# Five-product blocks of a gate and up projection: a bank of its own for the fourth product, ScalarE instead of VectorE on the running sum, and less urgent weights

## The chip, the cores and the metric

The kernel runs on one core of one Trainium2 chip. The metric is device time in microseconds (us) for one execution of the whole program. The core has a matrix engine (TensorE), a vector engine (VectorE, DVE in the rows), a scalar engine (ScalarE, ACT), GpSimd (POOL) and SyncE (SP), whose queue issues the DMAs. Matrix products land in PSUM, eight banks of 128 x 512 float32; everything else that is computed on lies in SBUF.

## The reference

Two layers of an encoder on x of 1024 tokens by 1024 features, all in float32. Each layer projects x, runs three groups of heads side by side (a gated linear recurrence, retention, and 2-D neighbourhood attention), projects their outputs back and normalises; then comes the part that the larger half of the change concerns:

```
hid = silu(x @ w_gate[l]) * (x @ w_up[l])
x = layer_norm(ALPHA * x + hid @ w_down[l])
```

w_gate and w_up are 1024 x 2816, that is 22 blocks of 128 hidden features. The other part of the change touches the recurrent group: six heads of 64 channels in three blocks of 128 channels, each with an x projection, a gate projection, a convolution of width four and two recurrences.

## The kernel before

**Products.** Each float32 matrix is split into an upper half, rounded to the matrix engine's float32r, and the rest; a product of two matrices is three matmuls (upper x upper, upper x rest, rest x upper). Each split is one ScalarE copy (`hi`, line 119) and one subtraction (`lo`, line 122) on VectorE, now and then on GpSimd.

**Gate and up.** `gate_up` computes x @ w_gate and x @ w_up by Strassen's scheme in Winograd's form, on 2 x 2 blocks: the token halves, the feature halves, and hidden blocks j and j + 11. So there are eleven pairs j, each with a w_gate and a w_up block, and each block has seven products of 12 matmuls (128 x 128 by 128 x 512). The left operands are sums of weight blocks: GpSimd forms them (`lefts`, line 902), ScalarE and VectorE split them into tiles `wsp`. The right operands B11, B21, B22, T1 to T4 are sums of quarters of x. In a name such as `w_gate<-T1h,wsp` the right operand tells the product: T2 is product 6, T3 is 7, T1 is 5, T4 is 4, B22 is 3.

For the first four pairs (`EARLY`) products 1 and 2 are done ahead, in `two`, while the last right operands are still being made; product 1 is kept in SBUF in `first[j]`, called `p1` in the rows. `rest` then does the last five products of these pairs, in the order 6, 7, 5, 4, 3, and all seven of pairs 4 to 10. In `rest`, products 6, 5 and 3 add up in one bank `z["a"]`, which is read in between:

```
p6: product 6 into a;         21 = p1 + a
p7: product 7 into d
p5: product 5 on to a;        22 = p1 + a; 22 = 22 + d
p4: product 4 on to d;        21 = 21 + d
p3: product 3 on to a;        12 = p1 + a
```

The additions are the `add` of line 1035, on VectorE. In pairs 4 to 10 product 1 is in bank a already, and 21 and 22 are copied out by ScalarE (line 1065). As each sum is complete, `done` hands it on: a gate's sum goes through a Silu on ScalarE (line 1136), an up's sum is multiplied with it on VectorE (line 1141, `hid`) and sent to DRAM. After the pair's last sum, four combinations for the down projection follow on VectorE (line 902, `hs` and `hid`). GpSimd also forms four sums of w_down per pair (line 1017, `qt`), sent to DRAM as `wt`.

**Order of work.** The program is traced as a list, and a planner then orders each engine's instructions beforehand: among those that it holds ready by its own estimate of durations, the one traced earliest goes first. `high_priority(offset=n)` makes instructions count as traced n earlier. Each engine then works through its list strictly in order. The weights of a block are prepared (`prep`) before the products of the block ahead of it are traced.

**Buffers.** PSUM has eight banks in rings: `mm` two (bank d), `mx` three (bank a), `mo` one, `ml` two. In SBUF, `W` has ten tiles (split weights, and `p1`), `wraw` four (loaded weights), `Q` four (GpSimd's sums), `S` eight (sums on their way, among others).

**The start of a layer.** `wload` loads a weight and splits it, the split with an urgency of `rush` = 400. `layer` runs `lru_main(0)` (x and gate projections of the recurrent group's block 0), in layer 1 between the last transposes and splits of x (`catch_up`, tiles `x2h` and `x2l`). It then weaves `lru_main(1)` with `lru_mix(0)`, whose first step is block 0's convolution (lines 326 to 329, tile `xc`, split into `xch` and `xcl`, which the gates' matmuls `lg` read), and `lru_main(2)` with `lru_mix(1)`; the weights of `w_rv` come next.

Of the kernel before, what the change touches and what calls it, by code (L numbers as in the profile page):

```python
# [11 lines left out]
AF = mybir.ActivationFunctionType  # L12
# [27 lines left out]
def weave(*lists):  # L40

    todo = []
    for n, st in enumerate(lists):
        st = [s if isinstance(s, tuple) else (1, s) for s in st]
        total, at = sum(c for c, _ in st), 0
        for i, (c, f) in enumerate(st):
            todo.append(((at + c / 2) / total, n, i, f))
            at += c
    for t in sorted(todo, key=lambda t: t[:3]):
        t[3]()  # L50


class Trunk:
    def __init__(self, ctx, tc, a):
        self.tc, self.nc, self.a = tc, tc.nc, a
        pool = lambda name, bufs, **kw: ctx.enter_context(tc.tile_pool(name=name, bufs=bufs, **kw))
        self.cp = pool("cp", 1)
        self.xp = pool("xp", 8)
        self.tp = pool("tp", 18)
        self.qp = pool("qp", 4)  # L60
        self.wp = pool("wp", 10)
        self.sp = pool("sp", 8)
        self.mp = pool("mp", 8)
        self.dp = pool("dp", 1, space=DRAM)
        self.pm = pool("pm", 1, space=PSUM)
        self.n = 0
        self.rush = 400
        self.rest = None


# [53 lines left out]
    def wload(self, src, n=1024):  # L124
        nc = self.nc
        raw = self.raw("wraw")
        nc.sync.dma_start(raw[:, :n], src)
        wh, wl = self.W("wh"), self.W("wl")
        with self.tc.high_priority(offset=self.rush):
            self.hi(wh[:, :n], raw[:, :n])  # L130
            self.lo(wl[:, :n], raw[:, :n], wh[:, :n])
        return wh, wl
# [661 lines left out]
    def layer(self, l):  # L794
        nc, tc, V, A = self.nc, self.tc, self.nc.vector, self.nc.scalar
        self.l = l
        ys = {}
        R, N, L = [{}, {}, {}], [{}, {}], [{}, {}, {}]
        m = self.lru_main(0, L[0])
        if l == 0:  # L800
            self.start(L[0])
            m = m[2:]
        for i, f in enumerate(m):
            f()
            self.catch_up(i)
        weave(self.lru_main(1, L[1]), self.lru_mix(0, L[0], ys))
        weave(self.lru_main(2, L[2]), self.lru_mix(1, L[1], ys))
        m = self.ret_main(0, R[0])
        weave(self.ret_v() + cost(0, [self.ret_tables]) + cost(2, m[:1]), cost(6, [lambda: None]) + self.lru_mix(2, L[2], ys))
        weave(m[1:])  # L810
        self.ret_tables2()
        weave(self.ret_main(1, R[1]), self.ret_mix(0, R[0], ys))
        if l == 0:
            self.bias()
        weave(self.ret_main(2, R[2]), self.ret_mix(1, R[1], ys))
        weave(self.na_v() + self.na_main(0, N[0]), self.ret_mix(2, R[2], ys))
        m = self.na_mix(0, N[0], ys)

        YH, YL = {}, {}
        ws = {}  # L820
        res = {}

        def ysplit(hf, i):
            def step():
                q, k = divmod(i, 4)
                if (hf, q) not in YH:
                    YH[hf, q], YL[hf, q] = self.X("yh"), self.X("yl")
                yh, yl = YH[hf, q][:, k, :], YL[hf, q][:, k, :]
                sl = slice(hf * 512, hf * 512 + 512)
                if i < 6:  # L830
                    t = self.S("yb")
                    nc.sync.dma_start(t, self.yd[i, :, sl])
                else:
                    t = ys[i][:, sl]
                self.hi(yh, t)
                self.lo(yl, t, yh)

            return step

        def load_res(tt):  # L840
            res[tt] = self.T("res")
            src = self.a["x"] if l == 0 else self.xd
            nc.sync.dma_start(res[tt], src[tt * P : (tt + 1) * P, :])

        def wout(chunks, evac):
            return [lambda tt=tt: wout_t(chunks, evac, tt) for tt in range(8)]

        def wout_t(chunks, evac, tt):
            if tt == 0:
                for i in chunks:  # L850
                    ws[i] = self.wload(self.a["w_out"][l, i * P : (i + 1) * P, :])
            hf, c = tt // 4, (tt % 4) * P
            if tt not in res:
                load_res(tt)
            for fh in range(2):
                ps = self.ps("wo", "mx" if fh and chunks is rest else "mm")
                f = slice(fh * 512, fh * 512 + 512)
                for j, i in enumerate(chunks):
                    for q, (y_, w_) in enumerate(((YH, 0), (YL, 0), (YH, 1))):
                        self.mm(ps, y_[hf, i // 4][:, i % 4, c : c + P], ws[i][w_][:, f], j == 0 and q == 0, j == len(chunks) - 1 and q == 2)  # L860
                evac(tt, f, ps)

        def ev0(tt, f, ps):
            with self.tc.high_priority(offset=self.rush):
                V.scalar_tensor_tensor(out=res[tt][:, f], in0=res[tt][:, f], scalar=ALPHA, in1=ps, op0=ALU.mult, op1=ALU.add)

        part, rest = (0, 1, 2, 3), (4, 5, 6, 7)
        wp = wout(part, ev0)
        nm = self.na_main(1, N[1])
        weave(nm[:2] + cost(0, [ysplit(0, i) for i in part]) + nm[2:] + wp[:2] + cost(0, [ysplit(1, i) for i in part]) + wp[2:6] + cost(0, [ysplit(hf, i) for hf in range(2) for i in (4, 5, 6)]) + wp[6:], m + self.na_mix(1, N[1], ys))  # L870
        for hf in range(2):
            for i in (7,):
                ysplit(hf, i)()
        g, b = self.gb(1)

        def ev1(tt, f, ps):
            with self.tc.high_priority(offset=self.rush):
                V.tensor_tensor(out=res[tt][:, f], in0=res[tt][:, f], in1=ps, op=ALU.add)
            if f.start:
                self.norm(res[tt], g, b, tt >= 4, tt < 7, then=lambda q: nc.sync.dma_start(self.x1d[tt * P : (tt + 1) * P, q], res[tt][:, q]))  # L880

        self.op = {}
        steps = wout(rest, ev1)
        for tt in range(8):
            steps[tt]()
            if tt == 7:
                self.settle()
            if tt >= 3:
                self.to_ops(tt - 3, res[tt - 3])
        self.gate_up([lambda t=t: self.to_ops(t, res[t]) for t in range(5, 8)])  # L890
        self.down()
# [84 lines left out]
    def gate_up(self, late):  # L976

        nc, l, V, A, G = self.nc, self.l, self.nc.vector, self.nc.scalar, self.nc.gpsimd
# [78 lines left out]
        def rest(name, j, w, done):  # L1057

            z = {}
            p1_ = first[j][:, NAMES.index(name), :] if j in first else None  # L1060

            def snap(n):
                z[n] = self.S(name + n)
                if p1_ is None:
                    A.activation(z[n], z["a"], AF.Copy)
                else:
                    add(z[n], p1_, z["a"])

            def p1():
                z["a"] = self.ps(name, "mx")  # L1070
                product(w, 1, z["a"], True)
                snap("11")

            def p2():
                b = self.ps(name, "mo")
                product(w, 2, b, True)
                add(z["11"], z["11"], b)
                done("11", z["11"])

            def p6():  # L1080
                if "a" not in z:
                    z["a"] = self.ps(name, "mx")
                product(w, 6, z["a"], p1_ is not None)
                snap("21")

            def p7():
                z["d"] = self.ps(name)
                product(w, 7, z["d"], True)

            def p5():  # L1090
                product(w, 5, z["a"], False)
                snap("22")
                add(z["22"], z["22"], z["d"])
                done("22", z["22"])

            def p4():
                product(w, 4, z["d"], False)
                add(z["21"], z["21"], z["d"])
                done("21", z["21"])

            def p3():
                product(w, 3, z["a"], False)
                if p1_ is not None:
                    snap("12")
                done("12", z.get("12", z["a"]))

            return ([p1, p2] if p1_ is None else []) + [p6, p7, p5, p4, p3]
# [309 lines left out]
```

## Time and profile before

| | |
|---|---|
| median of 3 runs | 2318.07 us (2317.54 to 2320.31) |
| the profiled execution | 2320.11 us |
| its span, first to last instruction | 2318.3 us |
| TensorE busy | 2241.5 us, 97% |
| VectorE, ScalarE, GpSimd busy | 1444.5, 983.9, 920.7 us |

A row of the profile names the line, the engine, the operation, the tile written and the tiles read, with their shapes. Matmuls are pipelined: one of 128 x 512 is shown with 0.39 us, while the next starts 0.23 us after it. Times of a row are microseconds from the start of the span.

### The profile page before, as it was taken

The page shows a single profiled execution, that of the slowest core. Times are in us where ns is not written, and L with a number is a line of the kernel's source. Part 1 is how long each engine was busy: PE and PEld are TensorE (multiplying, and loading weights), DVE is VectorE, ACT ScalarE, POOL GpSimd, SP SyncE. Part 2 cuts the span into 40 slices and gives each one's busy share as a digit, 9 for nine tenths or more (in the row PEclk, how much of TensorE's full clock was granted, in tenths as well). Part 3 has the DMA queues.
Part 4 walks back from the last instruction along what each step waited for, and adds up shares of the span by engine and source line. Part 5 has one row for each costly group of instructions (what it writes and reads, how often), then busy time and mean ns, then how long its engine had stood idle before and what let it go on. Part 6 is the DMA issues. An engine that isn't in the chain of part 4 may idle for free. (4 is left out here: it accounts for less than half of the span.)

```text
span 2318.3 us, 29337 instructions
## 1 busy us (share of the span) xinstructions
PE 2241.5 (97%) x10790; PEld 1811.2 (78%) x10790; DVE 1444.5 (62%) x2073; ACT 983.9 (42%) x1501; POOL 920.7 (40%) x568
## 2 busy tenths in 40 slices
PE   8999999999899999999989999999998999999998
PEld 6787877788678888888768878777876788888886
DVE  6966546588665666543658656456886665655336
ACT  5654355463223333444346533554632333343432
POOL 1425500045544343475513245001455443435655
PEclk9999999999999999999999999999999999999999
DMA  5232233324544445785321322333355454558742
GB/s 173 101 114 60 67 119 107 123 106 162 191 151 167 146 169 199 290 291 176 123 73 46 114 64 64 123 103 121 114 164 190 155 173 140 178 190 306 275 159 87
DMA packets 142697, 340.47 MB, mean 147 GB/s; under 512 B 24024, under 2 KB 37336, under 8 KB 142552
## 3 DMA queue, kind: packets, MB, share of 16 engines
q1 hardware_dynamic: 142552, 338.58, 43.4%
q8 instruction: 85, 1.39, 0.2%
q14 instruction: 60, 0.49, 0.1%
HBM read 242.88 MB, written 90.08 MB: 144 GB/s over the span
## 5 line engine op out<-in xcount | busy, mean ns | idle before, releaser
L116 PE MATMUL dn<-dw,hx 128*128 128x512 f32 x1848 | 420.7, 389 | 2.0 <-DVE dw L122 2.0
L116 PEld LDWEIGHTS dn<-dw,hx 128*128 128x128 f32 x1848 | 346.5, 188 | 74.3 <-DVE dw L122 2.4
L122 POOL TENSOR_TENSOR hx<-hraw,hx 128x1024 fp32r<-128x1024 f32 x80 | 206.5, 2597 | 196.6 <-ACT hx L119 193.1
L119 ACT ACTIVATE wsp<-qS 128x512 fp32r<-128x512 f32 x176 | 110.6, 631 | 276.0 <-PE w_up L116 136.1
L122 DVE TENSOR_TENSOR dw<-wraw,dw 128x1024 fp32r<-128x1024 f32 x84 | 122.5, 1464 | 159.4 <-ACT dw L119 149.7
L122 DVE TENSOR_TENSOR wsp<-qS,wsp 128x512 fp32r<-128x512 f32 x176 | 165.7, 942 | 65.6 <-ACT wsp L119 63.9
L119 ACT ACTIVATE dw<-wraw 128x1024 fp32r<-128x1024 f32 x84 | 83.1, 989 | 204.2 <-PE dn L116 188.0
L122 DVE TENSOR_TENSOR wl<-wraw,wh 128x1024 fp32r<-128x1024 f32 (+2 forms) x84 | 111.8, 1339 | 74.7 <-ACT wh L119 66.6
L119 ACT ACTIVATE wh<-wraw 128x1024 fp32r<-128x1024 f32 (+2 forms) x84 | 84.9, 1015 | 115.1 <-PE rk L116 27.7
L122 DVE TENSOR_TENSOR wsp<-wraw,wsp 128x512 fp32r<-128x512 f32 x100 | 110.7, 1110 | 23.0 <-ACT wsp L119 22.1
L902 POOL TENSOR_TENSOR qS<-wraw 128x512 f32<-128x512 f32 x44 | 65.0, 1477 | 142.6 <-DVE wsp L122 74.0
L119 ACT ACTIVATE wsp<-wraw 128x512 fp32r<-128x512 f32 x100 | 62.8, 630 | 129.9 <-PE w_up L116 81.0
L116 PE MATMUL wo<-wh,yh 128*128 128x512 f32 x256 | 103.0, 402 | 0.0
L116 PE MATMUL wo<-wl,yh 128*128 128x512 f32 x256 | 101.8, 398 | 0.0
L116 PE MATMUL wo<-wh,yl 128*128 128x512 f32 x256 | 100.7, 393 | 0.0
L1035 DVE TENSOR_TENSOR w_gate<-w_gate,w_gate 128x512 f32<-128x512 f32 x58 | 39.6, 682 | 91.2 <-PE w_gate L116 61.0
L119 ACT ACTIVATE hx<-hraw 128x1024 fp32r<-128x1024 f32 (+1 forms) x88 | 81.5, 940 | 16.6 <-DMA hraw<-hd 16.6
L642 POOL MEMSET tab<- 128x768 f32 x16 | 12.7, 794 | 182.0 <-DMA vd<-nv 46.9
L116 PE MATMUL w_gate<-T1h,wsp 128*128 128x512 f32 x176 | 64.5, 431 | 20.6 <-DVE w_gate L1035 17.3
L902 POOL TENSOR_TENSOR qS<-qS,wraw 128x512 f32<-128x512 f32 x44 | 67.3, 1529 | 41.0 <-issue 32.3
L902 POOL TENSOR_TENSOR qS<-wraw,wraw 128x512 f32<-128x512 f32 x44 | 60.7, 1379 | 57.3 <-DVE wsp L122 57.3
L1017 POOL TENSOR_TENSOR qt<-wraw 128x512 f32<-128x512 f32 x22 | 29.0, 1320 | 136.0 <-issue 122.1
(409 smaller groups left out, 6136.9 us busy)
## 6 DMA issues: line engine op xcount, KB each, us to landing
wraw<-in_w_down_dram SPq DMA_DIRECT2D x74, 512.0 KB
hraw<-hd SPq DMA_DIRECT2D x66, 512.0 KB
wraw<-in_w_gate_dram SPq DMA_DIRECT2D x52, 512.0 KB
wraw<-in_w_up_dram SPq DMA_DIRECT2D x52, 512.0 KB
wt<-qt SPq DMA_DIRECT2D x88, 256.0 KB
hd<-hid SPq DMA_DIRECT2D x80, 256.0 KB
wraw<-wt SPq DMA_DIRECT2D x40, 512.0 KB
wraw<-in_w_st_dram SPq DMA_DIRECT2D x36, 512.0 KB
```

The source lines that it names most:

```text
L116: return self.nc.tensor.matmul(out, lhsT=lhsT, rhs=rhs, start=start, stop=stop, skip_group_check=more)
L119: return self.nc.scalar.activation(out, src, AF.Copy, scale=scale)
L122: return (eng or self.nc.vector).tensor_tensor(out=out, in0=src, in1=hi.bitcast(F32), op=ALU.subtract)
L642: self.order(nc.gpsimd.memset(t, NEG), self.mark)
L902: t = lambda o, x, y, op: eng.tensor_tensor(out=o, in0=x, in1=y, op=op)
L1017: t = lambda o, x, y: G.tensor_tensor(out=o, in0=x, in1=y, op=ALU.subtract)
L1035: add = lambda o, x, y: V.tensor_tensor(out=o, in0=x, in1=y, op=ALU.add)
```

## The change

In the five-product form of `rest` (pairs 0 to 3 of each layer):

- the sum after product 6 and the one after product 5 are copied out of bank a by ScalarE without p1;
- p1 is added to bank d after product 7, on VectorE, into a new tile q of the ring `S`, and q is then added to 22 and to 21;
- product 4 starts a bank of its own, the one called `mo`, and 21 takes in q and then that bank;
- 12 = p1 + a stays on VectorE.

Besides, `wload` takes its urgency from a new number, `rushw`, which is 40 instead of 400 while `lru_main(1)` and `lru_mix(0)` are traced; for all other weights it stays at 400.

```diff
-        self.rush = 400
+        self.rush = self.rushw = 400
...
-        with self.tc.high_priority(offset=self.rush):
+        with self.tc.high_priority(offset=self.rushw):
             self.hi(wh[:, :n], raw[:, :n])
             self.lo(wl[:, :n], raw[:, :n], wh[:, :n])
...
+        self.rushw = 40
         weave(self.lru_main(1, L[1]), self.lru_mix(0, L[0], ys))
+        self.rushw = 400
         weave(self.lru_main(2, L[2]), self.lru_mix(1, L[1], ys))
...
             def snap(n):
                 z[n] = self.S(name + n)
-                if p1_ is None:
-                    A.activation(z[n], z["a"], AF.Copy)
-                else:
-                    add(z[n], p1_, z["a"])
+                A.activation(z[n], z["a"], AF.Copy)
...
             def p6():
-                if "a" not in z:
+                if p1_ is not None:
                     z["a"] = self.ps(name, "mx")
                 product(w, 6, z["a"], p1_ is not None)
                 snap("21")
...
             def p7():
                 z["d"] = self.ps(name)
                 product(w, 7, z["d"], True)
+                if p1_ is not None:
+
+                    z["q"] = self.S("q")
+                    add(z["q"], p1_, z["d"])

             def p5():
                 product(w, 5, z["a"], False)
                 snap("22")
-                add(z["22"], z["22"], z["d"])
+                add(z["22"], z["22"], z["d"] if p1_ is None else z["q"])
                 done("22", z["22"])

             def p4():
-                product(w, 4, z["d"], False)
-                add(z["21"], z["21"], z["d"])
+                if p1_ is None:
+                    product(w, 4, z["d"], False)
+                    add(z["21"], z["21"], z["d"])
+                else:
+                    e = self.ps(name, "mo")
+                    product(w, 4, e, True)
+                    add(z["21"], z["21"], z["q"])
+                    add(z["21"], z["21"], e)
                 done("21", z["21"])

             def p3():
                 product(w, 3, z["a"], False)
                 if p1_ is not None:
-                    snap("12")
+                    z["12"] = self.S(name + "12")
+                    add(z["12"], p1_, z["a"])
                 done("12", z.get("12", z["a"]))
```

## Rows read from the trace of the kernel before

**Rows 1.** The page: busy time of each engine, its share of the span, instructions.

```profile
PE 2241.5 (97%) x10790; PEld 1811.2 (78%) x10790; DVE 1444.5 (62%) x2073; ACT 983.9 (42%) x1501; POOL 920.7 (40%) x568
```

**Rows 2.** Busy time by stretch: engines with instruction counts, granted clock, DMA share, GB/s.

```profile
544.00:676.30 132.30, 120.82 (x494) 94.18 (x493) 91.18 (x108) 34.54 (x56) 71.50 (x50) 0.96 0.54 177
676.30:700.00 23.70, 22.08 (x97) 17.65 (x96) 14.90 (x21) 10.20 (x18) 7.64 (x6) 1.00 0.35 129
700.00:938.00 238.00, 238.00 (x1044) 193.66 (x1043) 145.82 (x173) 89.33 (x149) 98.95 (x71) 1.00 0.50 170
1701.00:1833.20 132.20, 121.44 (x505) 95.21 (x504) 92.69 (x112) 36.56 (x59) 72.13 (x50) 0.97 0.54 179
1833.20:1860.00 26.80, 25.18 (x111) 20.25 (x110) 15.97 (x21) 10.16 (x18) 11.96 (x9) 1.00 0.43 147
618.80:652.50 33.70, 30.30 (x121) 23.45 (x121) 23.37 (x28) 8.64 (x14) 18.25 (x13) 0.95 0.57 190
585.40:588.90 3.50, 3.50 (x10) 2.75 (x9) 0.00 (x0) 0.00 (x0) 1.27 (x1) 0.51 0.72 218
```

**Rows 3.** TensorE's waits in 544:664 (first), 1700:1860 (second), 664:938 (third).

```profile
PE w_gate L116 <- DVE w_gate L1035: 8.7, 3, 3.6
PE w_up L116 <- DVE w_up L1035: 2.0, 4, 0.7
...
PE w_up L116 <- DVE w_up L1035: 2.1, 5, 0.5
...
PE w_gate L116 <- ACT w_gate L1065: 1.6, 1, 1.6
PE w_up L116 <- DVE w_up L1035: 0.8, 2, 0.4
```

**Rows 4.** Timeline 572:592: start, duration, then idle time before it and its releaser.

```profile
573.11 0.69 DVE L122 TENSOR_TENSOR wsp<-qS,wsp 128x512 fp32r<-128x512 f32 x1
...
573.72 0.69 DVE L1141 TENSOR_TENSOR hid<-w_gate,w_up 128x512 f32<-128x512 f32 x1
...
576.24 1.61 POOL L902 TENSOR_TENSOR qS<-wraw 128x512 f32<-128x512 f32 x1 [0.68 <-DVE wsp L122]
...
576.63 1.77 DVE L122 TENSOR_TENSOR wsp<-qS,wsp 128x512 fp32r<-128x512 f32 x1
...
584.11 0.67 DVE L1035 TENSOR_TENSOR w_gate<-p,w_gate 128x512 f32<-128x512 f32 x1
...
584.84 0.50 PE L116 MATMUL w_gate<-T1h,wsp 128*128 128x512 f32 x1 [3.65 <-DVE w_gate L1035]
...
589.54 0.63 ACT L119 ACTIVATE wsp<-qS 128x512 fp32r<-128x512 f32 x1 [7.91 <-PE w_gate L116]
```

**Rows 5.** Durations (min/median/max, ns) at line 1035; groups of VectorE in 572:664.

```profile
L1035 DVE TENSOR_TENSOR w_gate<-w_gate,w_gate x58: 671/686/689, 554.1 to 2078.7; 128x512 f32<-128x512 f32 x58
...
L122 DVE TENSOR_TENSOR wsp<-qS,wsp 128x512 fp32r<-128x512 f32 x23 | 23.9, 1038 | 0.7 <-ACT wsp L119 0.3
```

**Rows 6.** Timeline of ScalarE, 674:692, in the first late pair.

```profile
686.59 0.63 ACT L1136 ACTIVATE w_gate<-w_gate 128x512 f32<-128x512 f32 x1 [3.75 <-DVE w_gate L1035]
...
687.64 0.58 ACT L1065 ACTIVATE w_gate<-w_gate 128x512 f32<-128x512 f32 x1
```

**Rows 7.** Starts of the layers: TensorE's waits, VectorE's and SP's timeline, matmuls of w_rv.

```profile
PE lg L116 <- ACT xch L119: 2.8, 1, 2.8
...
28.77 2.35 DVE L122 TENSOR_TENSOR wl<-wraw,wh 128x1024 fp32r<-128x1024 f32 x2
...
30.02 1.46 SPq L127 DMA_DIRECT2D wraw<-in_w_rv_dram  x2
...
L116 PE MATMUL w_rv<-wh,xh x64: 333/334/660, 94.8 to 140.2; 128*128 128x384 f32 x64
...
PE xt L787 <- DVE x2l L122: 6.9, 3, 4.1
...
1161.81 3.64 DVE L122 TENSOR_TENSOR wl<-wraw,wh 128x1024 fp32r<-128x1024 f32 x2
```

## The prediction

> **What bounds the kernel now.** I read the page's table of engines first: TensorE is busy 97% of the span and nothing else is above 78% [rows 1]. So only time in which TensorE does not issue matmuls at its full rate can be won, and the question is where that time lies. The table of windows gives the yardstick. In the late pairs of gate and up (700 to 938 us) 1044 matmuls take 238.0 us, 0.228 us each [rows 2]. By that price the five-product part of layer 0 (544.0 to 676.3 us) holds 494 x 0.228 = 112.6 us of matmuls and lasts 132.3: 19.7 us are lost. In layer 1 (1701.0 to 1833.2) it is 505 x 0.228 = 115.1 of 132.2: 17.1 lost. Together 36.8 us, nearly half of what TensorE loses in the whole run (2318.3 less 2241.5 busy is 76.8).
>
> The view of TensorE's waits says for whom: VectorE at line 1035, the `add` of sums, with 8.7 + 2.0 us in layer 0, 8.7 + 2.1 in layer 1, and 0.8 just behind layer 0's [rows 3], 22.3 in all. The timeline of one such wait shows the cause [rows 4]. Product 7 of the gate block has ended, VectorE is in a burst (hidden products and the four combinations of line 902 of the pair before, with weight splits between them), and the add that reads the bank of product 6 (line 1035, 584.11) comes at its end. Product 5, which adds on to that bank, may not start before it, and TensorE sits idle 3.65 us. Right after it TensorE runs slowly: the granted clock is 0.51 from 585.4 to 588.9, that is the lower level of 1.2 GHz, after this idle stretch; full clock would have spared about half of those 3.5 us, 1.7. There are five such stretches (three in layer 0, two in layer 1; the first is shown), 8.5 us. The rest of the 36.8, 6.0 us, is what each stop costs beyond the idle time named: the last matmul drains and the weight load starts anew.
>
> While TensorE stands, ScalarE does nothing: after the wait its next instruction shows 7.91 us of idle time [rows 4]. In a period of 33.7 us, from one such wait to the next (618.8 to 652.5), ScalarE is busy 8.6 us, VectorE 23.4, GpSimd 18.3 [rows 2].
>
> **The change part by part.** *The copy.* In the eight five-product blocks of a layer the read of the bank after product 6, and after product 5, goes from VectorE (0.68 us, at the end of its burst) to ScalarE as a plain copy. The row of this copy in the late pairs is 0.58 us (line 1065) [rows 6]. Two per block, 16 blocks in both layers: 32 x 0.58 = 18.6 us more on ScalarE, 2.3 per pair, on an engine that has 25 of 33.7 us free. Queued behind a copy are the upper halves of the next weights and the Silus; a copy that waits for TensorE holds them up by as long.
>
> *The fourth product's own bank.* Product 4 no longer adds on to the bank of product 7, so it needn't wait for the two adds that follow product 5. That wait is part of the 2.0 and 2.1 us of w_up above. The bank is the single one called `mo`. It is free once the last add of the block has read it, and the next block needs it five products on: 60 x 0.228 = 13.7 us later, longer than VectorE's burst of 11.1 us (573.72 to 584.78) [rows 4].
>
> *VectorE's adds.* There were five per block and there are five again (q, two on 21, one on 22, one on 12), so it isn't relieved. But two of them now read two SBUF tensors (z22 + q and z21 + q) where all five read one from PSUM. The adds with a PSUM input take 671 to 689 ns in every one of their rows [rows 5]. The weight splits of the same width with two SBUF inputs take 1038 ns on average in 572 to 664, one of them 0.69 us (573.11), another 1.77 us (576.63, while GpSimd works from 576.24 on) [rows 4, 5]. So the four moved adds of a pair cost between nothing and 4 x (1.77 - 0.69) = 4.3 us more; I take 4 x (1.04 - 0.68) = 1.4, the average of that split. A pair's VectorE work goes from about 23.4 us [rows 2] to 24.8, in a period that would be 120 x 0.228 = 27.4 us without waits. It fits, at 91%.
>
> The Trainium skill speaks against the change here: the GPSIMD Engine Reference, section Key points, says that GpSimd shares its SBUF interfaces with VectorE, in contention with VectorE instructions that have two SBUF inputs. The rows agree: 1.77 us beside GpSimd's instruction, and 0.69 us for the same form three microseconds before. If the rule struck all four adds every time, the sum would be that of the second rival below; by the mean of the rows it's hidden.
>
> *What remains of the waits.* The form with a ScalarE copy already runs in the late pairs, which gives both bounds. From 700 to 938 us TensorE loses nothing. In the first late pair, though, product 5 waits 1.6 us for line 1065 [rows 3]: the copy (687.64) is behind a Silu (686.59) which waited 3.75 us for a VectorE add behind the burst [rows 6]. With the restart that is 97 x 0.228 = 22.1 against 23.7 us in 676.3 to 700, so 1.6 lost, and 111 x 0.228 = 25.3 against 26.8, so 1.5 in layer 1 [rows 2]. For 16 blocks: 0 to 16 x 1.6 = 25.6 us. In the early pairs a gate block has no Silu ahead of its first copy (sum 11 was done earlier), so it is nearer to the late pairs without loss; an up block has the gate's three Silus ahead of its copies. I take six of the 16 blocks at 1.6: 9.6 us. The losses of the first late pairs (1.6 + 1.5) have the same burst ahead of them, and I leave them as they are.
>
> So gate and up give 36.8 - 9.6 = 27.2 us.
>
> *The weights of block 1 (rushw).* Only the splits that are queued while `lru_main(1)` is traced lose their urgency: for each of two weights one ScalarE upper half and one VectorE rest, per layer. Their loads keep their place in the SP queue, but their raw buffers (four) come free later, and the loads of w_rv, next in that queue (30.02 us), with them; w_rv is first multiplied at 94.8 us, which covers it [rows 7]. In layer 0 two splits (2.35 us) stand between the second and third step of the convolution, and TensorE waits 2.8 us for the convolution's upper half. In layer 1 two splits (3.64 us) stand just ahead of the x2l splits for which TensorE waits 6.9 us in three places [rows 7]. What speaks against a full gain: the weights of block 2 stay at the old urgency, so they may now go first and fill the place. I count one split of 1.2 us out of the way in each layer, 2.4. The bounds are -2.4 (block 1's own splits come late, one per layer) and 2.8 + 6.9 = 9.7 (all these waits).
>
> *The sum.* The profiled execution took 2320.1 us, its span 2318.3. 2320.1 - 27.2 - 2.4 = 2290.5. The median of the three runs is 2.0 below the profiled one, so 2288.5; I predict 2288. With gate and up at their best, the first late pairs too, 36.8 + 3.1 + 2.4 = 42.3 go, which gives 2276.
>
> **The rivals.** *ScalarE's queue takes over.* Every copy, not six, is caught behind something late, a Silu or a weight that waits for its buffer, as in the first late pair. Then 25.6 us stay: 36.8 - 25.6 + 2.4 = 13.6 gained, 2304. For it: ScalarE's order is fixed beforehand, and that row shows what a late Silu does to it [rows 6]. Against it: the late pairs from 700 us on.
>
> *VectorE becomes the bound.* With all four adds at 1.77 a pair has 23.4 + 4.3 = 27.7 us. GpSimd's 18.3 us in 27.4 instead of 33.7 make it a neighbour for 67% of the time rather than 54%; the lengthening of the ten weight splits, now 10 x (1.04 - 0.68) = 3.6 us, grows by a quarter, 0.9. Then 28.6 is above 27.4, by 1.2 us in each of eight pairs: 9.6, and the time is 2298.
>
> *Slower.* The ring of small tiles (`S`, eight buffers) holds sums, q and the last combination: 3 + 3 + 1 = 7 per pair before, 4 + 4 + 1 = 9 now. If the copy after product 6 must wait for a buffer that only VectorE's burst sets free, product 5 waits as it did, and ScalarE's queue with the next weights stands as well. The 36.8 us stay, and each of the 16 blocks loses a further 1.6: 2318 + 26 = 2344 at worst, about 2330 if half of them do. It decides as soon as the buffer comes free later than the end of product 7, 2.7 us behind product 6. Against it: the hidden products that free six of the buffers stand at the head of the burst (first at 573.72) [rows 4].
>
> *No change.* The planner, which orders each engine's instructions beforehand, fills the place with other work and product 5 comes as late as before: 2318.
>
> **How the numbers follow.** My forecast (2276 to 2297) 0.56; VectorE as the bound 0.13; ScalarE's queue 0.17; nothing 0.06; slower 0.08. The two middle cases, with some of both, reach from 2298 to about 2312, so 2276 to 2312 holds 0.86; the bounds of the other costs make it no narrower. A change of 0.2% (4.6 us) is about what a measurement of this kernel can tell: faster 0.86, same 0.06, slower 0.08.
>
> **What would show it.** Right: in 544 to about 660 no TensorE wait for VectorE at the `add` line before product 5, no stretch at half clock, 0.23 us per matmul, a pair every 27 to 28 us. VectorE above 90% there, with the two SBUF adds near 1 us. ScalarE copies of 0.58 us within 2 us of product 6's end. Wrong: a TensorE wait for the ScalarE copy in most blocks (first rival); VectorE without idle time and weight splits that reach TensorE late (second); a ScalarE copy that waits for VectorE's hidden product (third). At the layers' starts the splits of two weights should stand behind the convolution and the x2l splits; if others stand there in their place, that part gave nothing.

## The result and the profile after

The changed kernel takes 2279.42 us, median of 5 runs (2274.94 to 2284.74); the kernel before took 2320.31 (5 runs, 2317.54 to 2321.49). The ratio is 0.9829, with a 95% interval of 0.9816 to 0.9841: 41 us won. The forecast was 2288, 30 us below the 2318.07 that the kernel before had then shown. The execution that was profiled is the slowest of the five, 2284.74 us, with a span of 2283.0.

First the page of the changed kernel, its table of engines, to be held against [rows 1]:

```profile
PE 2228.8 (98%) x10790; PEld 1808.8 (79%) x10790; DVE 1468.7 (64%) x2073; ACT 998.0 (44%) x1533; POOL 932.0 (41%) x568
```

ScalarE has 32 instructions more, the 32 copies, and 14 us more busy time. The time that TensorE loses (span less busy) went from 76.8 to 54.2 us.

The table of windows of the changed kernel: the five-product part with the first late pair in layer 0, the same in layer 1, and one pair of layer 0. Columns as in [rows 2].

```profile
546.40:683.00 136.60, 133.23 (x582) 108.28 (x581) 116.88 (x127) 50.89 (x89) 81.19 (x56) 1.00 0.59 192
1681.50:1819.00 137.50, 134.55 (x587) 109.37 (x587) 116.57 (x128) 51.51 (x90) 83.30 (x56) 1.00 0.58 191
579.30:608.30 29.00, 27.56 (x121) 22.45 (x120) 24.89 (x28) 10.28 (x20) 18.84 (x14) 1.00 0.62 200
```

By the prediction's yardstick of 0.228 us, 582 matmuls are 132.7 of 136.6 us and 587 are 133.8 of 137.5: 3.9 and 3.7 us lost, where the kernel before lost 36.8 + 3.1 in the same part of the work. The granted clock is 1.00 in both. In the pair shown VectorE has 24.89 us of work in 29.00.

TensorE's waits of the changed kernel, in 546 to 683 us (first two lines) and 1681 to 1820 (last two); the columns are those of [rows 3]:

```profile
PE w_gate L116 <- ACT w_gate L1066: 3.0, 3, 1.5
PE w_up L116 <- ACT w_up L1066: 0.3, 1, 0.3
...
PE w_gate L116 <- ACT w_gate L1066: 2.5, 3, 1.0
PE w_up L116 <- ACT w_up L1066: 0.3, 1, 0.3
```

No wait for VectorE's `add` is left, where there were 22.3 us of them [rows 3]. TensorE waits for ScalarE's copy (line 1066) eight times, 6.1 us: in six of the 16 early blocks, two gate and one up in each layer, and in the first late gate block of each layer (0.7 us each, where the kernel before had 1.6).

**Where the rest went.** One length can be read in every kernel here: from the first matmul of the first pair's product 6 to the last of product 2 in the first late pair, called the pairs below. Before it is 156.07 us in layer 0 (from 544.10) and 153.40 in layer 1 (from 1701.10), now 138.17 and 137.74: 33.6 us less. The starts of the layers give 5.8 and 4.5 us more, read from the places of the same matmuls in the two traces, ahead of each start and behind it. That is 43.9, but the two spans differ by 35.3, because in this execution 8.8 us were lost again between 160 and 274 us, where no wait of the change lies. The changed kernel was run once more, beside other experiments (2277.64 us, 2274.72 to 2281.67, ratio 0.9804, 0.978 to 0.9829), expected at 2275 to 2282, most of this loss being that one execution's own. So it was: its profiled execution does not have that loss, and its span is 2274.2, 44.1 us below that of before. The same stretch in the table of windows, first the changed kernel's first execution, then the second's:

```profile
160.00:274.00 114.00, 105.52 (x598) 82.78 (x598) 69.46 (x87) 37.04 (x59) 56.65 (x37) 0.94 0.23 65
```

```profile
160.00:274.00 114.00, 108.52 (x682) 87.13 (x681) 72.04 (x92) 45.17 (x72) 62.91 (x41) 1.00 0.25 75
```

The clock is 0.94 in one and 1.00 in the other, with the same instructions: at the first, TensorE ran stretches at 1.2 GHz (from 173.1, 200.4 and 258.5 us, behind waits of 1.7, 1.5 and 2.2 us). So in what follows only the pairs and the starts are compared, each for itself.

At the start of layer 0 VectorE's timeline of the changed kernel shows the convolution's steps (lines 326 to 329) between the weight splits:

```profile
28.29 1.22 DVE L122 TENSOR_TENSOR wl<-wraw,wh 128x1024 fp32r<-128x1024 f32 x1
...
30.77 2.36 DVE L122 TENSOR_TENSOR wl<-wraw,wh 128x1024 fp32r<-128x1024 f32 x2
...
34.86 1.27 DVE L329 SCALAR_TENSOR_TENSOR xc<-xs,convw,xc 128x1023 f32<-128x1023 f32 x1
36.05 1.21 DVE L122 TENSOR_TENSOR wl<-wraw,wh 128x1024 fp32r<-128x1024 f32 x1
```

Before, two more splits were ahead of the last step, five from 28.77 us on instead of three, and it began later:

```profile
38.20 1.27 DVE L329 SCALAR_TENSOR_TENSOR xc<-xs,convw,xc 128x1023 f32<-128x1023 f32 x1
```

TensorE's waits at the starts, layer 0 and then layer 1 (2.8 and 6.9 us in [rows 7]):

```profile
PE lg L116 <- ACT xch L119: 1.2, 1, 1.2
...
PE xt L787 <- DVE x2l L122: 1.0, 1, 1.0
```

At the start of layer 1 the wait shrank because of three splits of weights that stood ahead of the sixth x2l split (the two from 1161.81 on [rows 7] and one before them) two come later; one still stands there. VectorE's timeline of the changed kernel:

```profile
1144.93 1.21 DVE L122 TENSOR_TENSOR wl<-wraw,wh 128x1024 fp32r<-128x1024 f32 x1
...
1153.51 2.35 DVE L122 TENSOR_TENSOR wl<-wraw,wh 128x1024 fp32r<-128x1024 f32 x2
```

In layer 0 more went than the difference of the waits. Before, TensorE ran at half clock behind the waits for the convolution's halves, and now it does not. The same stretch in the windows, before and after:

```profile
42.70:49.60 6.90, 5.93 (x14) 4.68 (x15) 0.92 (x1) 3.05 (x4) 0.00 (x0) 0.51 0.00 0
```

```profile
42.70:49.60 6.90, 6.90 (x31) 5.51 (x30) 2.45 (x2) 6.62 (x8) 0.45 (x1) 1.00 0.00 0
```

### The profile page after: what moved, and what is told of

Its sections match the earlier page's. It is cut to its first block, busy times and chain, and to the rows that moved or that the text cites. A ratio compares the mean times of both kernels' runs of the same rounds, so it can differ in the third digit from the quotient of the medians.

```text
span 2283.0 us, 29389 instructions
## 1 busy us (share of the span) xinstructions
PE 2228.8 (98%) x10790; PEld 1808.8 (79%) x10790; DVE 1468.7 (64%) x2073; ACT 998.0 (44%) x1533; POOL 932.0 (41%) x568
## 5 line engine op out<-in xcount | busy, mean ns | idle before, releaser
L122 DVE TENSOR_TENSOR wsp<-qS,wsp 128x512 fp32r<-128x512 f32 x176 | 171.1, 974 | 77.5 <-ACT wsp L119 76.1
L122 DVE TENSOR_TENSOR wl<-wraw,wh 128x1024 fp32r<-128x1024 f32 (+2 forms) x84 | 107.2, 1284 | 77.6 <-ACT wh L119 72.8
L904 POOL TENSOR_TENSOR qS<-wraw 128x512 f32<-128x512 f32 x44 | 67.9, 1542 | 137.5 <-DVE wsp L122 68.4
L119 ACT ACTIVATE hx<-hraw 128x1024 fp32r<-128x1024 f32 (+1 forms) x88 | 81.5, 940 | 17.4 <-DMA hraw<-hd 17.3
L642 POOL MEMSET tab<- 128x768 f32 x16 | 12.7, 795 | 182.0 <-DMA vd<-nv 47.0
L516 POOL TENSOR_TENSOR qd<-rq,qw 64x512 f32<-64x512 f32 x48 | 70.9, 1476 | 23.1 <-PE var L116 8.4
L502 DVE SCALAR_TENSOR_TENSOR st<-st,gch 64x64 f32<-64x64 f32 x144 | 64.2, 497 | 22.1 <-ACT st L490 20.6
```

The source lines that it names most:

```text
L119: return self.nc.scalar.activation(out, src, AF.Copy, scale=scale)
L122: return (eng or self.nc.vector).tensor_tensor(out=out, in0=src, in1=hi.bitcast(F32), op=ALU.subtract)
L502: V.scalar_tensor_tensor(out=t(m), in0=t(s), scalar=self.gch[d * 64 : d * 64 + 64, 2 * pr + h : 2 * pr + h + 1], in1=t(m), op0=ALU.mult, o ...
L516: self.mark = G.tensor_tensor(out=blk(t, P)[d * 64 : d * 64 + 64, :, :], in0=blk(z["rq"][hp, sl], P), in1=self.qw[hp, pr : pr + 1, d, :].t ...
L642: self.order(nc.gpsimd.memset(t, NEG), self.mark)
L904: t = lambda o, x, y, op: eng.tensor_tensor(out=o, in0=x, in1=y, op=op)
```

## The experiments

Theory A, that of the prediction: product 5 waits because the read of the running bank stands behind VectorE's burst; read by ScalarE it is on time. Its rivals are named with each run. All results, with the length of the pairs in both layers added up (before 309.5, after 275.9 us):

| kernel | median us (range) | ratio (95%) | pairs, us | against before |
|---|---|---|---|---|
| after, again | 2277.64 (2274.72 to 2281.67) | 0.9804 (0.978 to 0.9829) | 275.5 | -34.0 |
| blocks_alone | 2290.95 (2286.45 to 2297.95) | 0.9865 (0.9838 to 0.9892) | 275.0 | -34.4 |
| urgency_alone | 2308.45 (2307.27 to 2312.61) | 0.9941 (0.9919 to 0.9962) | 309.0 | -0.5 |
| copies_same_bank | 2295.99 (2294.5 to 2296.95) | 0.9885 (0.9862 to 0.9909) | 283.8 | -25.6 |
| bank_alone | 2306.81 (2302.65 to 2312.47) | 0.9932 (0.9905 to 0.9959) | 295.1 | -14.4 |
| fourth_before_fifth | 2304.9 (2300.16 to 2307.75) | 0.9918 (0.9894 to 0.9943) | 299.5 | -10.0 |
| copies_urgent | 2285.18 (2279.95 to 2288.42) | 0.9833 (0.9808 to 0.9859) | 278.1 | -31.3 |
| urgency_both | 2286.95 (2285.0 to 2290.1) | 0.984 (0.9814 to 0.9867) | 275.4 | -34.0 |
| sum22_direct | 2280.06 (2278.47 to 2287.45) | 0.9817 (0.9788 to 0.9846) | 278.4 | -31.1 |
| five_sum_buffers | 2278.67 (2274.76 to 2281.36) | 0.9808 (0.9779 to 0.9838) | 279.7 | -29.8 |

The kernel before took 2323.7, 2322.03 and 2321.97 us in the three groups of runs (the first four, the next four with "after, again", the last two).

**blocks_alone and urgency_alone: the two parts by themselves.** The first drops the line `self.rushw = 40` from the changed kernel; the second is the kernel before with the edits to `rush` and `rushw` alone.

> The whole change of the five-product blocks, with the weights' urgency left at 400 everywhere. Theory A (the time came from product 5's waits for VectorE and from the half clock behind them): the five-product parts give what the trace of the changed kernel shows for them, 18.2 us in layer 0 and 16.0 in layer 1, so 34 us less than before, about 2286; the starts of the layers are as before (TensorE waits 2.8 us for the convolution's upper half and 6.9 us for the x2l splits). Theory B (the urgency of the weights made more than half of the gain, and the blocks follow from it): less than 20 us, above 2300.

> The kernel before, with the lower urgency of block 1's weights alone. Theory A: the start of layer 0 gives 4 to 6 us and that of layer 1 about 4.5, as in the trace of the changed kernel, and between 160 and 274 us up to 8.8 us may go again, so 2 to 10 us less than before (2310 to 2318); the waits at product 5 are all there. Theory B: 20 us or more. A third possibility, that the loss between 160 and 274 us follows from the urgency itself and always takes all of layer 0's gain: 2 us less than before at most in layer 0 and 4.5 in layer 1, about 2316.

The blocks give 34.4 us in the pairs and leave the waits at the starts as they were, as theory A expected. The urgency gives 11.0 us over the whole trace (15 by the medians), a little more than the 2 to 10 expected, and leaves the waits in the pairs. TensorE's waits of blocks_alone, then of urgency_alone, whole run:

```profile
PE xt L787 <- DVE x2l L122: 6.9, 3, 4.1
PE w_gate L116 <- ACT w_gate L1065: 4.7, 6, 1.0
...
PE lg L116 <- ACT xch L119: 2.8, 1, 2.8
```

```profile
PE w_gate L116 <- DVE w_gate L1037: 18.4, 6, 3.7
...
PE w_up L116 <- DVE w_up L1037: 5.2, 13, 0.6
```

34.4 + 11.0 is 45.4, and the second execution of the whole change shows 44.1. Since single executions differ by several us, this says that the parts add up roughly; that neither works through the other is shown by the waits, which each part leaves where it does not reach.

**copies_same_bank and bank_alone: which half of the blocks' edit does it.** The first keeps ScalarE's copies (and the old urgency) but lets product 4 add on to the bank of product 7 as before. The second is the kernel before with product 4 in the bank `mo` and nothing else.

```
         if p1_ is None:                       # copies_same_bank
             ...
         else:
-            e = self.ps(name, "mo")
-            product(w, 4, e, True)
-            add(z["21"], z["21"], z["q"])
-            add(z["21"], z["21"], e)
+            product(w, 4, z["d"], False)
+            add(z["21"], z["21"], p1_)
+            add(z["21"], z["21"], z["d"])
```

> As blocks_alone, but product 4 adds on to the bank of product 7, which VectorE has read into q by then; 21 takes in p1 and then that bank, so the number of VectorE's adds is the same. Theory A (with q, product 4 has nothing to wait for, and a bank of its own is worth nothing): within 3 us of blocks_alone. Rival (product 4's own bank carries part of the gain): its waits come back, 0.7 us and a restart in up to 16 blocks, 5 to 16 us more than blocks_alone.

> The kernel before, with a bank of its own for product 4 and nothing else: the sums after products 6 and 5 stay with VectorE, there is no q, and 21 takes in two banks, one VectorE add more per block (0.68 us). Theory A: the waits at product 5 stay (17.4 us named, five stretches at half clock), or grow by the added add; only product 4's waits go, 3 to 5 us: 2314 to 2322. Rival (the bank was the point): 20 us less than before, below 2300.

Theory A fell in both; of the rivals, that of copies_same_bank came out in size (5.0 us more by the medians, 8.8 in the pairs), and that of bank_alone did not. With the copies alone, product 5 is on time but product 4 is not. TensorE's waits of copies_same_bank, whole run:

```profile
PE w_gate L116 <- DVE q L1036: 12.5, 6, 2.9
```

The add that makes q reads the bank of product 7 on VectorE, and it too stands at the end of the burst; product 4, which adds on to that bank, waits for it. So the own bank is worth 34.4 - 25.6 = 8.8 us beside the copies. Without the copies the bank is worth 14.4, more than the 3 to 5 us expected. TensorE's timeline of bank_alone shows what moved:

```profile
576.38 0.39 PE L116 MATMUL w_gate<-T3h,wsp 128*128 128x512 f32 x1
576.61 0.39 PE L116 MATMUL w_gate<-T4h,wsp 128*128 128x512 f32 x1
...
577.52 0.39 PE L116 MATMUL w_gate<-T4l,wsp 128*128 128x512 f32 x1
581.92 0.79 PE L116 MATMUL w_gate<-T1h,wsp 128*128 128x512 f32 x1 [4.01 <-DVE w_gate L1035]
```

Product 4 (T4), which now depends on nothing that is read, was in part put ahead of product 5 (T1). The wait, for the add at the end of the burst, stays, and the first matmul after it takes 0.79 us, at half clock. The waits of bank_alone, whole run, then all those in its pairs of layer 0 (543 to 692 us), then one of the kernel before in 1700 to 1860:

```profile
PE w_gate L116 <- DVE w_gate L1035: 17.6, 6, 4.0
...
PE w_gate L116 <- DVE w_gate L1035: 9.0, 3, 4.0
...
PE w_gate L116 <- ACT w_gate L1065: 1.6, 1, 1.6
```

So the waits at product 5 of the gate blocks are as long as before (17.4). What went are the others in the pairs: those of the up blocks for the `add` (2.0 + 0.8 and 2.1 us [rows 3]) and those for the copy in the first late pairs (1.6 in each layer), 8.1 us by name. How the other 6.3 us came about is not shown.

**fourth_before_fifth: give the copy more time by order.** The changed kernel with the early blocks' products as 6, 7, 4, 5, 3, so that 2.7 us more lie between the copy's source and product 5.

```
-            return ([p1, p2] if p1_ is None else []) + [p6, p7, p5, p4, p3]
+            return [p1, p2, p6, p7, p5, p4, p3] if p1_ is None else [p6, p7, p4, p5, p3]
```

> The changed kernel with the five products in the order 6, 7, 4, 5, 3: product 4, which has a bank of its own and needs no sum, stands between the copy after product 6 and product 5. Theory A (the rest of the waits at product 5, 5.5 + 0.6 us named in the changed kernel, is a copy that comes up to 1.5 us late, and 2.7 us of other matmuls cover it): those waits go, 3 to 8 us less than the changed kernel. Rival (product 3 then waits for the second copy, which has nothing between it and product 5 any more): the waits move to product 3, no gain or up to 8 us more.

It loses most of the gain, far more than the 8 us that its rival allowed, and shows the mechanism of the prediction's first rival nearly at full price, though in eight gate blocks (six early, two first late). Its waits, whole run; then ScalarE's and TensorE's timelines:

```profile
PE w_gate L116 <- ACT w_gate L1066: 22.8, 8, 4.9
```

```profile
584.15 0.63 ACT L1146 ACTIVATE w_gate<-w_gate 128x512 f32<-128x512 f32 x1 [6.67 <-DVE w_gate L1037]
584.68 0.58 ACT L1066 ACTIVATE w_gate<-w_gate 128x512 f32<-128x512 f32 x1
```

```profile
585.32 0.79 PE L116 MATMUL w_gate<-B22h,wsp 128*128 128x512 f32 x1 [4.94 <-ACT w_gate L1066]
```

With product 4 early, sum 21 is complete early, its Silu (line 1146) is put ahead of the second copy in ScalarE's order, and that Silu waits 6.67 us for a VectorE add behind the burst. The copy after product 5 waits with it, and product 3 (B22) for the copy.

**copies_urgent: move the copies ahead in ScalarE's order.** In the changed kernel the copies are issued under `high_priority(offset=self.rush)`, as the weights are.

> The changed kernel with the ScalarE copies counted as traced 400 earlier. Theory A (the copies come late because ScalarE's queue holds upper halves of weights ahead of them that wait for GpSimd's sums): the copies stand one or two weights earlier, the 6 us of waits shrink, 2 to 6 us less than the changed kernel. Rival (a copy that stands early makes ScalarE wait for TensorE, and the next weights come late): same or more.

No gain: the waits for the copies are 8.1 us in eight places instead of 5.5 in six (gate blocks, whole run), and the pairs are 2.2 us longer. But in the gate blocks the copies hardly moved: the first copy of a block stands behind four or five splits of weights in both kernels. In the block with the longest wait of the changed kernel (below) it is behind the same four here:

```profile
599.91 0.63 ACT L119 ACTIVATE wsp<-qS 128x512 fp32r<-128x512 f32 x1 [2.43 <-POOL qS L904]
...
602.12 0.58 ACT L1067 ACTIVATE w_gate<-w_gate 128x512 f32<-128x512 f32 x1
```

In the up blocks one split fewer is ahead of it, and their waits are gone. So what a gate's copy ahead of the splits would give was not tried.

**urgency_both: the same low urgency for the weights of the next block too.** The line `self.rushw = 400` moves below the second `weave`.

> The changed kernel with the urgency of 40 for block 2's weights too. Theory A (in the changed kernel three splits still stand ahead of the convolution's third step, and block 2's take the place that block 1's left): the convolution comes 1 to 2.5 us earlier in layer 0, and nothing changes at x2l, where one split is left: 1 to 3 us less. Rival (weights of block 2 come too late for their matmuls): TensorE waits for a weight, more time.

No gain: the pairs are the same. The convolution's last step does come 1.0 us earlier, but the start of layer 0 gets worse (the wait `lg` for `tg` 3.2 us, 1.7 before this edit; a stretch at half clock at 80.9): at 133 us the matmuls are 2.3 us ahead of their places in the trace of before, where the changed kernel is 6.4 ahead.

**What is the remaining wait?** ScalarE's timeline of the changed kernel at its longest, then GpSimd's, then TensorE's:

```profile
602.54 0.64 ACT L119 ACTIVATE wsp<-qS 128x512 fp32r<-128x512 f32 x1 [5.22 <-POOL qS L904]
605.61 0.63 ACT L119 ACTIVATE wsp<-qS 128x512 fp32r<-128x512 f32 x1 [2.44 <-POOL qS L904]
...
607.81 0.58 ACT L1066 ACTIVATE w_gate<-w_gate 128x512 f32<-128x512 f32 x1
```

```profile
599.47 1.66 POOL L904 TENSOR_TENSOR qS<-wraw 128x512 f32<-128x512 f32 x1 [1.36 <-DMA wt<-qt]
```

```profile
608.44 0.50 PE L116 MATMUL w_gate<-T1h,wsp 128*128 128x512 f32 x1 [1.46 <-ACT w_gate L1066]
```

Product 6 ended 12 matmuls, 2.7 us, before product 7, so near 604; the copy begins at 607.81, behind weight splits that waited 5.22 and 2.44 us for GpSimd's sums, and GpSimd had waited for a transfer. Four of the eight waits are of this kind, in early gate blocks, 0.8 to 1.5 us each, behind splits that waited for GpSimd or VectorE. In the other four, two up blocks (0.3 us each) and the two first late gate blocks (0.7 each), a Silu that waited for a VectorE add stands ahead of the copy. ScalarE's timeline, layer 0:

```profile
617.76 0.63 ACT L1146 ACTIVATE w_gate<-w_gate 128x512 f32<-128x512 f32 x1 [5.13 <-DVE w_gate L1037]
...
622.00 0.58 ACT L1066 ACTIVATE w_up<-w_up 128x512 f32<-128x512 f32 x1
...
669.36 0.63 ACT L1146 ACTIVATE w_gate<-w_gate 128x512 f32<-128x512 f32 x1 [3.79 <-DVE w_gate L1037]
...
670.42 0.58 ACT L1066 ACTIVATE w_gate<-w_gate 128x512 f32<-128x512 f32 x1
```

Two runs tried to get round the waits. One lets VectorE make sum 22 by one add of q and the bank, with no copy after product 5; one gives the ring of GpSimd's sums five buffers instead of four.

```
         product(w, 5, z["a"], False)          # sum22_direct
-        snap("22")
-        add(z["22"], z["22"], z["d"] if p1_ is None else z["q"])
+        if p1_ is None:
+            snap("22")
+            add(z["22"], z["22"], z["d"])
+        else:
+            z["22"] = self.S(name + "22")
+            add(z["22"], z["q"], z["a"])
...
-        self.qp = pool("qp", 4)               # five_sum_buffers
+        self.qp = pool("qp", 5)
```

> The changed kernel, but 22 is formed by one VectorE add of q and the bank after product 5, in place of ScalarE's copy and an add of two SBUF tensors. It takes 0.86 to 1.39 us (the means of those adds) minus 0.68 from VectorE per block and one copy from ScalarE; product 3 then waits for VectorE, with product 4's 2.7 us between. Theory A (a read of the running bank on VectorE stands at the end of its burst, wherever it is): TensorE waits for VectorE again, now ahead of product 3, as the kernel before did ahead of product 5, less the 2.7 us: 1 to 3 us in the eight gate blocks, so 5 to 20 us more than the changed kernel. Rival (VectorE's two-SBUF adds were what held the rest up): 2 to 6 us less.

> The changed kernel with five buffers instead of four in the ring Q of GpSimd's sums. Theory A (what is left at product 5 is a copy behind an upper half that waits for GpSimd, which waits for a sum buffer until its DMA has landed): the 5.5 us of waits for the copy shrink to 2 or less, 3 to 5 us less. Rival (the ring only moves the wait: GpSimd, at work more closely, lengthens VectorE's instructions): within 2 us.

Neither can be told from the changed kernel by its time. TensorE's waits of sum22_direct in 530 to 690, then of five_sum_buffers there:

```profile
PE w_gate L116 <- DVE w_gate L1037: 4.4, 3, 2.5
```

```profile
PE w_up L116 <- ACT w_up L1066: 3.1, 3, 1.7
PE w_gate L116 <- ACT w_gate L1066: 2.8, 3, 1.4
```

With one VectorE instruction less and no second copy, the wait comes back at VectorE for product 3, which adds on to the same bank: the direction of theory A, but 2.4 us more in the pairs and not 5 to 20. A fifth buffer does not shrink the waits as its theory A expected: it lengthens those of the up blocks and leaves about as much in the gate blocks, and the pairs are 3.8 us longer. What would remove the last 6 us stays open. None of these versions beats the changed kernel.

## Why the prediction was right

**What bounded the kernel, and the copy: right.** In the five-product parts the waits for the `add` are gone, as are the half-clock stretches, and the gain is there with the blocks' edit alone. ScalarE's copy takes 0.58 us, as its row in the late pairs had it [rows 6]. The lengths of ScalarE's rows add up to 18.5 us more than before, 18.6 forecast; busy time grew by only 14 because rows lie partly over each other.

**The residual (9.6 us kept): too high.** Including the first late pairs, the prediction left 36.8 + 3.1 - 27.2 = 12.7 us lost; 3.9 + 3.7 = 7.6 are. It took six blocks at 1.6 each, after the first late pair's copy behind a late Silu. Six blocks it is, but no row gave that number, so this is luck; they wait 6.1 - 2 x 0.7 = 4.7 us, 0.8 each, and the first late blocks wait less too. It also had the blocks the wrong way round: it looked for the waits in the up blocks, behind the gate's Silus, where they are 0.3 us in two blocks, and held the gate blocks to be nearly free, where four copies are late by 0.8 to 1.5 us behind splits of weights. The Silu costs as much as was feared only when product 4 goes first (fourth_before_fifth). The first rival's mechanism, a copy behind something late, is present in six blocks and not in all 16, at half the price.

**The own bank: right edit, wrong size.** The prediction took it to be worth part of 2.0 + 2.1 us. Those waits do go with the bank alone. But they were read off a trace in which product 4 of a gate block had no wait at all, coming after product 5's long one. With product 5 on time, the next reader of a running bank at the end of the burst (q) would have cost 8.8 us. The same reasoning, that a running bank is better read early or not at all, applied one product further on, and the prediction did not apply it.

**VectorE's adds: within the bounds.** The changed kernel's groups of VectorE, 573 to 660 us (busy, mean ns, then idle time before):

```profile
L1037 DVE TENSOR_TENSOR w_up<-w_up,q 128x512 f32<-128x512 f32 x6 | 8.3, 1386 | 0.1
L1037 DVE TENSOR_TENSOR w_gate<-w_gate,q 128x512 f32<-128x512 f32 x6 | 5.0, 861 | 0.0
```

The 12 adds with two SBUF inputs have a mean of (8.3 + 5.0) / 12 = 1.11 us against 1.04 forecast, so 1.7 us more per pair than at 0.68, against 1.4. Over both layers they take 675 to 1781 ns (durations min/median/max):

```profile
L1037 DVE TENSOR_TENSOR w_gate<-w_gate,q x16: 675/679/1777, 554.8 to 1779.4; 128x512 f32<-128x512 f32 x16
L1037 DVE TENSOR_TENSOR w_up<-w_up,q x16: 678/1625/1781, 567.1 to 1790.1; 128x512 f32<-128x512 f32 x16
```

Those with a PSUM input stay at 671 to 690. The eleven longest of the 32, 1.62 us and more, run beside GpSimd instructions for at least 0.69 of their length, and the eleven that run beside none take 0.68; but some of the short ones, too, run beside GpSimd. That agrees with the rule of the Trainium skill that the prediction weighed (GPSIMD Engine Reference, Key points), though not for every add. The second rival stood on VectorE having no room: in the pair shown it has 24.89 us of work (24.8 forecast) in 29.00, and TensorE waits for none of it there. Two signs came out beside their mark: VectorE is busy 86% and not above 90%, and a pair takes 27.5 to 28.9 us instead of 27 to 28, because of the waits that are left.

**The urgency: the sign right, the size too small.** 2.4 us were forecast, within -2.4 to 9.7; the starts gave 10.3 (and 11.0 over the whole trace alone). Two things were mis-sized. In layer 1 two splits, not one, moved out of the way of the x2l splits that TensorE waited for, and 5.9 of 6.9 us of waiting went; other waits near them grew by 1.1, and 4.5 were gained. And in layer 0 the half clock from 42.7 to 49.6 went with the waits, which no term held: 31 matmuls instead of 14 are recorded in that stretch. Block 2's weights did not take the whole place, as was feared, though one of their splits still stands there in layer 0: with urgency_both two splits and not three are ahead of the convolution's last step.

**The others.** The ring of small tiles and the planner were given 0.08 and 0.06; in no row does a copy itself wait for VectorE, as it would for a buffer that the burst frees. The copies of the gate blocks in 546 to 683 us, with the idle time before them and what ended it:

```profile
L1066 ACT ACTIVATE w_gate<-w_gate 128x512 f32<-128x512 f32 x11 | 6.4, 584 | 7.8 <-PE w_gate L116 7.8
```

The errors point one way: 5.1 us in the residual and 7.9 at the starts, together 13.0 more than the 29.6 that were taken off the profiled execution. That is 42.6, and the second profiled execution of the changed kernel gained 44.1. The measured medians give 41 and 44.

## What to carry to other kernels

A product that adds on to a bank after somebody has read it waits for that reader's place in its queue, so the read belongs on an engine whose queue is short there; and when one such read is moved, look for the next one, which the first wait had hidden. Where that engine also carries work that depends on the long queue (here the Silus), its order decides: swapping two products cost 24 us of 34. A wait that lowers TensorE's clock costs more than its own time, so the price of a short wait at a layer's start includes the clock of the stretch behind it.

## What was not expected of the hardware

The stretches at 1.2 GHz are not a fixed property of a kernel: with the same instructions, the clock between 160 and 274 us was 0.94 in one profiled execution and 1.00 in another, and by the position of the same matmuls against the trace of before, the first stood at +2.4 us at the end of it and the second at -7.2. The same matmul waits 1.74 us for GpSimd in the one (171.92 us) and 1.75 in the other (171.73); then the windows are these, first execution and second:

```profile
173.10:176.50 3.40, 3.40 (x9) 2.63 (x10) 3.03 (x4) 1.36 (x4) 3.26 (x4) 0.51 0.02 5
```

```profile
173.10:176.50 3.40, 3.40 (x16) 2.81 (x15) 3.22 (x4) 1.18 (x4) 3.32 (x3) 1.00 0.00 0
```

So the length of a wait alone does not tell here what the clock does after it. Most of the spread from 2274.9 to 2284.7 us can be of this kind: the mean granted clock of the slowest of the five runs is 0.993 and that of the fastest 0.996, by my estimate some 7 of the 9.8 us. What sets off the one or the other stays open.
